# Softmax with a relative position bias, streamed through SBUF: chunks of 7 rows in three buffers and a 3-row spare instead of chunks of 6 rows in four

## The chip, the cores and the metric

The kernel runs on one core of a Trainium2 chip. The metric is the device time of one execution in microseconds, given as the median of several runs. The profile is a record of one execution, taken by the hardware profiler.

## What is computed

```python
B, H, S, max_rel = 2, 8, 2112, 16
rel = clip(pos[:, None] - pos[None, :], -max_rel, max_rel) + max_rel
logits = logits + rel_bias[:, rel][None]          # (B, H, S, S) float32
exp = np.exp(logits - logits.max(axis=-1, keepdims=True))
return exp / exp.sum(axis=-1, keepdims=True)      # (B, H, S, S) float32
```

To every row of a 2112 x 2112 matrix of logits a bias is added that depends only on the distance between row and column, and each row then goes through a softmax. There are 16 such matrices, 285 MB of input and as much of output.

## The kernel before

**Layout.** The 2 x 8 x 2112 rows are shared out over 128 partitions: `ROWS = 264` consecutive rows to each. A row has `S = 2112` float32 numbers, 8,448 bytes. A chunk is `R = 6` rows of every partition (6,336 KB in all, 50,688 contiguous bytes per partition), held in one of `NBUF = 4` buffers `X0` to `X3`. There are 44 chunks; chunk n lives in buffer n mod 4, and it is computed in place and stored from the same buffer.

**The bias.** ACT's DMA queue loads the table `rel_bias`, broadcast to all partitions (L97, 132 KB, into F). VectorE selects each partition's head and builds from it the long strip `M` in PSUM (L118 to L155). The bias of one row is a window of `M` that slides by one element from row to row. Once per round of four chunks VectorE copies the part of `M` that the round needs into the tile `F` in SBUF (`strip`, L160), and the adds read shifted windows of `F`.

**VectorE.** For each chunk it waits for the load's semaphore and then runs for each row one custom operation (L166): it adds the bias and leaves the negative maximum of the row. Then it waits for the exponentials of half a chunk, takes the reciprocals of their sums (L183) and scales the rows (L187), half a chunk at a time. It does not begin the next chunk's adds before that.

**ScalarE** computes the exponential of each row with the sum of the row beside it (L175), as soon as the row is added.

**SP** issues all large transfers, on one DMA queue, in a fixed order: at the start the first chunk as six transfers of one row (L88; five of them count on the semaphore `pre`, for which VectorE waits before the first `strip`, L190), and three whole chunks; then store 0; then in a loop for each chunk

```python
store(j + (b + 1) * R, (b + 1) % NBUF)   # waits until the rows of that chunk are scaled
take(nc.sync, st[b], 16)                 # waits until the store before it has landed
load(j + (b + NBUF) * R, b)              # into the buffer that came free
```

so the load of chunk c+4 goes out once store c has landed and store c+1 has been issued. At the end three stores, the last chunk's in two halves of 3 rows, and a wait for all of them. Line L74 is the helper `take`, through which all engines wait, L78 the helper `load`, L82 the helper `store`.

Of the kernel before, what the change touches and what calls it, by code (L numbers as in the profile page):

```python
# [7 lines left out]
FP32 = mybir.dt.float32  # L8
I32 = mybir.dt.int32
EXP = mybir.ActivationFunctionType.Exp  # L10
ALU = mybir.AluOpType
ENG = mybir.EngineType
# [3 lines left out]
def kernel(  # L16
# [6 lines left out]
    nc = tc.nc  # L23
    P = 128
    B, H, S, S2 = logits.shape
# [3 lines left out]
    ROWS = B * H * S // P  # L29
    PB = S // ROWS  # L30
    assert ROWS * P == B * H * S and PB * ROWS == S and PB == H == 8
    R = 6
    NBUF = 4
    STEP = R * NBUF
    N = ROWS // R
    HALF = R // 2
    assert ROWS % STEP == 0
    MW = S + ROWS - 1
    FW = S + STEP - 1
    BIG = 3.0e38  # L40

    io = ctx.enter_context(tc.tile_pool(name="io", bufs=1))
    X = [io.tile([P, R * S], FP32, tag=f"X{b}", name=f"X{b}") for b in range(NBUF)]
    F = io.tile([P, FW], FP32, tag="F", name="F")
    rbS = io.tile([P, W], FP32, tag="rbS", name="rbS")
    nmax = io.tile([P, STEP], FP32, tag="nmax", name="nmax")
    tot = io.tile([P, STEP], FP32, tag="tot", name="tot")
    rec = io.tile([P, STEP], FP32, tag="rec", name="rec")
    ip = io.tile([P, 3, PB], I32, tag="ip", name="ip")
    ps = ctx.enter_context(tc.tile_pool(name="ps", bufs=1, space=bass.MemoryType.PSUM))  # L50
    M = ps.tile([P, 4096], FP32, tag="M", name="M")

    def view(t, offset, dims):

        return bass.AP(tensor=t.tensor, offset=t.offset + offset, ap=[[list(t.ap[0])[0], P]] + dims)

    def rows(t, j, n):

        return bass.AP(tensor=t.tensor, offset=t.offset + j * S, ap=[[ROWS * S, P], [1, n * S]])

    with tc.tile_critical(no_gpsimd_drain=True):
        ld = [nc.alloc_semaphore(f"ld{b}") for b in range(NBUF)]
        st = [nc.alloc_semaphore(f"st{b}") for b in range(NBUF)]
        added = nc.alloc_semaphore("added")
        expd = nc.alloc_semaphore("expd")
        scaled = nc.alloc_semaphore("scaled")
        inv = nc.alloc_semaphore("inv")
        rb = nc.alloc_semaphore("rb")
        pre = nc.alloc_semaphore("pre")
        idx = nc.alloc_semaphore("idx")  # L70
        dve = nc.alloc_semaphore("dve")

        def take(eng, sem, n):
            eng.wait_ge(sem, n).then_inc(sem, -n)  # L74


        def load(j, b):
            nc.sync.dma_start(out=X[b][:, :], in_=rows(logits, j, R)).then_inc(ld[b], 16)  # L78

        def store(j, b, s0=0, n=R):  # L80
            take(nc.sync, scaled, n)
            nc.sync.dma_start(  # L82
                out=rows(out, j + s0, n), in_=X[b][:, s0 * S : (s0 + n) * S]
            ).then_inc(st[b], 16)


        for r in range(R):
            nc.sync.dma_start(  # L88
                out=X[0][:, r * S : (r + 1) * S], in_=rows(logits, r, 1)
            ).then_inc(ld[0] if r == R - 1 else pre, 16)  # L90
        for n in range(1, NBUF):
            load(n * R, n)

        rbB = view(F, 0, [[1, H * W]])
        nc.scalar.dma_start(  # L97
            out=rbB,
            in_=bass.AP(tensor=rel_bias.tensor, offset=rel_bias.offset, ap=[[0, P], [1, H * W]]),
# [4 lines left out]
        v = nc.vector  # L104
        done = [0]

        def then(ins):
            done[0] += 1
            ins.then_inc(dve, 1)

        def settle():
            v.wait_ge(dve, done[0])

        SC = H * W
        mask = [F[:, SC + i * PB : SC + (i + 1) * PB] for i in range(9)]
        dp, dh, eq, hm, gt, le, lt, ra, rz = mask
        v.wait_ge(idx, 2)
        then(v.tensor_scalar(out=ip[:, 1], in0=ip[:, 0], scalar1=3, scalar2=7,  # L118
                             op0=ALU.logical_shift_right, op1=ALU.bitwise_and))
# [7 lines left out]
        for m, op in ((eq, ALU.is_equal), (gt, ALU.is_gt), (le, ALU.is_le), (lt, ALU.is_lt)):  # L127
# [3 lines left out]
        then(v.tensor_tensor(  # L131
            out=view(F, 0, [[W, H], [1, W]]), in0=view(F, 0, [[W, H], [1, W]]),
            in1=view(F, SC + 3 * PB, [[1, H], [0, W]]), op=ALU.mult))
        settle()
        then(v.tensor_reduce(out=rbS[:, :], in_=view(F, 0, [[1, W], [W, H]]),  # L135
                             axis=mybir.AxisListType.X, op=ALU.add))
        settle()
# [3 lines left out]
        then(v.tensor_tensor(  # L141
            out=view(F, 0, [[W, PB], [1, W]]), in0=view(F, SC + 2 * PB, [[1, PB], [0, W]]),
            in1=view(rbS, W - 1, [[0, PB], [-1, W]]), op=ALU.mult))
# [6 lines left out]
            out=view(M, U, [[ROWS, PB], [1, W]]), in0=view(F, 0, [[W, PB], [1, W]]),  # L150
            in1=view(F, SC + 8 * PB, [[1, PB], [0, W]]), op=ALU.add))
        then(v.tensor_copy(out=view(M, U + W, [[ROWS, PB], [1, ROWS - W]]),  # L152
                           in_=view(F, SC + 7 * PB, [[1, PB], [0, ROWS - W]])))
# [1 line left out]
        then(v.tensor_copy(out=M[:, U + PB * ROWS : MW], in_=high.to_broadcast([P, MW - U - PB * ROWS])))  # L155
        settle()

        def strip(j):

            v.tensor_copy(out=F[:, :], in_=M[:, bass.ds(ROWS - STEP - j, FW)]).then_inc(dve, 1)  # L160

        def add(b):
            take(v, ld[b], 16)
            for r in range(b * R, (b + 1) * R):
                x = X[b][:, (r - b * R) * S : (r - b * R + 1) * S]
                v.tensor_tensor_reduce(  # L166
                    out=x, in0=x, in1=F[:, STEP - 1 - r : STEP - 1 - r + S], scale=-1.0, scalar=BIG,
                    op0=ALU.add, op1=ALU.min, accum_out=nmax[:, r : r + 1],
                ).then_inc(added, 1)

        def exps(b):
            for r in range(b * R, (b + 1) * R):
                x = X[b][:, (r - b * R) * S : (r - b * R + 1) * S]
                take(nc.scalar, added, 1)
                nc.scalar.activation(  # L175
                    out=x, in_=x, func=EXP, scale=-1.0, bias=nmax[:, r : r + 1],
                    accum_out=tot[:, r : r + 1],
                ).then_inc(expd, 1)

        def scale(b):  # L180
            for r0 in range(b * R, (b + 1) * R, HALF):
                take(v, expd, HALF)
                v.reciprocal(out=rec[:, r0 : r0 + HALF], in_=tot[:, r0 : r0 + HALF]).then_inc(inv, 1)  # L183
                take(v, inv, 1)
                for r in range(r0, r0 + HALF):
                    x = X[b][:, (r - b * R) * S : (r - b * R + 1) * S]
                    v.tensor_scalar_mul(out=x, in0=x, scalar1=rec[:, r : r + 1]).then_inc(scaled, 1)  # L187

        v.sem_inc(dve, -done[0])
        take(v, pre, 16 * (R - 1))  # L190
        with nc.Fori(0, ROWS - STEP + 1, STEP, engines=[ENG.DVE]) as j:  # L191
            strip(j)
            take(v, dve, 1)
            for b in range(NBUF):
                add(b)
                scale(b)
        with nc.Fori(0, ROWS // STEP, 1, engines=[ENG.Activation]):
            for b in range(NBUF):
                exps(b)

        store(0, 0)
        with nc.Fori(0, ROWS - 2 * STEP + 1, STEP, engines=[ENG.SP]) as j:
            for b in range(NBUF):
                store(j + (b + 1) * R, (b + 1) % NBUF)
                take(nc.sync, st[b], 16)
                load(j + (b + NBUF) * R, b)
        for n in range(N - NBUF + 1, N - 1):
            store(n * R, n % NBUF)  # L210
        store((N - 1) * R, (N - 1) % NBUF, 0, HALF)
        store((N - 1) * R, (N - 1) % NBUF, HALF, R - HALF)
        for b in range(NBUF):
            take(nc.sync, st[b], 32 if b == (N - 1) % NBUF else 16)


# [28 lines left out]
```

## Time and profile before

| | |
|---|---|
| median of 3 runs | 1330.84 us (1330.0 to 1331.05) |
| span of the profiled execution | 1327.7 us |
| median less this span | 3.1 us |
| VectorE busy | 976.6 us (74%) |
| ScalarE busy | 575.2 us (43%) |
| read and written in HBM | 285.61 and 285.47 MB, 430 GB/s over the span |
| packets on all DMA queues | 13,683 |

The profile's times are microseconds from the start of the span. DVE is VectorE, ACT ScalarE, SPq and ACTq are the sequencers that issue transfers. A line of the timeline gives start, duration, engine, line of code, operation, output and input, and in brackets how long the engine was idle before it and what ended that. A line on a DMA queue gives its packets, its megabytes and the time its packets took as a share of 16 engines' time. A line of a window gives the window, its length, busy time of VectorE, ScalarE and GpSimd, the TensorE clock, the share of busy DMA engines and GB/s. TensorE is not used.

### The profile page before, as it was taken

Reading aid. Unit: us, or ns where it says so; the run is one execution under the profiler, and the core shown is the slowest. Engines: PE = TensorE matmul, PEld = TensorE weight load, DVE = VectorE, ACT = ScalarE, POOL = GpSimd, SP = SyncE. Lnnn points to the kernel's source line nnn. Section 1 sums busy time; section 2 is a strip of 40 time slices with the busy share of each in tenths; the row PEclk is TensorE's granted clock in tenths of the full one; section 3 lists DMA queues with packets and bytes.
Section 4 is the critical chain, followed back from the end, with each engine's and each line's share of the span. In section 5 each row is a group of like instructions: output and inputs, shape, how many; then the busy total and the mean of one; then the engine's idle time right before and its main releaser. Section 6 shows DMA issues by size and latency. Waiting matters only on the chain. (4 is left out here: it accounts for less than half of the span.)

```text
span 1327.7 us, 2454 instructions
## 1 busy us (share of the span) xinstructions
DVE 976.6 (74%) x911; ACT 575.2 (43%) x539; POOL 0.4 (0%) x6
## 2 busy tenths in 40 slices
DVE  6999667777777776687778777677877776687772
ACT  2564333444444343345444333444444343335440
POOL 0000000000000000000000000000000000000000
DMA  9999999999999999999999999999999999999998
GB/s 392 431 428 437 435 420 437 435 434 425 435 437 434 428 435 434 435 429 429 438 438 432 426 438 437 437 425 437 437 437 425 435 440 437 428 432 438 437 426 359
DMA packets 13683, 571.11 MB, mean 430 GB/s; under 512 B 1521, under 2 KB 1649, under 8 KB 1649
## 3 DMA queue, kind: packets, MB, share of 16 engines
q1 hardware_dynamic: 13536, 570.96, 99.6%
q10 hardware_dynamic: 144, 0.14, 0.1%
q14 instruction: 3, 0.02, 0.0%
HBM read 285.61 MB, written 285.47 MB: 430 GB/s over the span
## 5 line engine op out<-in xcount | busy, mean ns | idle before, releaser
L166 DVE CUSTOM_DVE_ANT_0 X<-X,F 128x2112 f32<-128x2112 f32 x264 | 605.2, 2354 | 301.3 <-DVEq L74 301.3
L175 ACT ACTIVATE X<-X,nmax 128x2112 f32<-128x2112 f32 x264 | 541.7, 2052 | 539.3 <-ACTq L74 517.6
L187 DVE TENSOR_SCALAR X<-X,rec 128x2112 f32<-128x2112 f32 x264 | 332.4, 1315 | 13.2
L175 ACT ACT_TABLE_LOAD x11 | 14.1, 1283 | 183.3 <-ACTq L74 183.3
L175 ACT ACTIVATION_READ_ACCUMULATOR X<-X,nmax 128x1 f32 x264 | 49.2, 186 | 0.0
L160 DVE COPY F<-M 128x2135 f32 x11 | 26.1, 2374 | 6.3 <-DVEq L74 6.3
L166 DVE DVE_READ_ACCUMULATOR2_ANT nmax<- 128x1 f32 x264 | 21.7, 82 | 0.0
L183 DVE RECIPROCAL rec<-tot 128x3 f32<-128x3 f32 x88 | 14.9, 170 | 0.0
L131 DVE TENSOR_TENSOR F<-F 128x264 f32<-128x264 f32 x1 | 0.4, 434 | 4.7 <-DMA F<-in_rel_bias_dram 4.7
L152 DVE COPY M<-F 128x1848 f32<-128x1848 f32 x1 | 2.1, 2077 | 0.0
L118 DVE TENSOR_SCALAR ip<-ip 128x8 int32<-128x8 int32 x1 | 0.2, 173 | 1.3 <-POOL ip L102 1.3
L135 DVE TENSOR_REDUCE rbS<-F 128x33 f32<-128x264 f32 x1 | 0.6, 610 | 0.0
L149 DVE TENSOR_TENSOR M<-F 128x264 f32<-128x264 f32 x1 | 0.4, 441 | 0.0
L141 DVE TENSOR_TENSOR F<-F,rbS 128x264 f32<-128x264 f32 x1 | 0.4, 425 | 0.0
L128 DVE TENSOR_SCALAR F<-F 128x8 f32<-128x8 f32 x4 | 0.4, 166 | 0.0
L154 DVE COPY M<-rbS 128x247 f32<-128x247 f32 x1 | 0.4, 408 | 0.0
L139 DVE TENSOR_SCALAR F<-F,rbS 128x8 f32<-128x8 f32 x1 | 0.2, 231 | 0.0
L145 DVE SCALAR_TENSOR_TENSOR F<-F,rbS 128x8 f32<-128x8 f32 x1 | 0.2, 225 | 0.0
L140 DVE TENSOR_SCALAR F<-F,rbS 128x8 f32<-128x8 f32 x1 | 0.2, 222 | 0.0
L146 DVE SCALAR_TENSOR_TENSOR F<-F,rbS 128x8 f32<-128x8 f32 x1 | 0.2, 219 | 0.0
L124 DVE TENSOR_TENSOR F<-ip 128x8 f32<-128x8 int32 x1 | 0.2, 167 | 0.0
L121 DVE TENSOR_TENSOR F<-ip 128x8 f32<-128x8 int32 x1 | 0.2, 166 | 0.0
(9 smaller groups left out, 1.2 us busy)
## 6 DMA issues: line engine op xcount, KB each, us to landing
X<-in_logits_dram SPq DMA_DIRECT2D x43, 6336.0 KB, 44.6
out_dram<-X SPq DMA_DIRECT2D x43, 6336.0 KB, 52.6
X<-in_logits_dram SPq DMA_DIRECT2D x6, 1056.0 KB, 12.1
out_dram<-X SPq DMA_DIRECT2D x2, 3168.0 KB, 21.1
F<-in_rel_bias_dram ACTq DMA_DIRECT2D x1, 132.0 KB, 6.2
```

Of the source, the lines that this page charges most:

```text
L128: then(v.tensor_scalar(out=m, in0=dp, scalar1=0.0, scalar2=None, op0=op))
L131: then(v.tensor_tensor(out=view(F, 0, [[W, H], [1, W]]), in0=view(F, 0, [[W, H], [1, W]]), in1=view(F, SC + 3 * PB, [[1, H], [0, W]]), op= ...
L135: then(v.tensor_reduce(out=rbS[:, :], in_=view(F, 0, [[1, W], [W, H]]), axis=mybir.AxisListType.X, op=ALU.add))
L141: then(v.tensor_tensor(out=view(F, 0, [[W, PB], [1, W]]), in0=view(F, SC + 2 * PB, [[1, PB], [0, W]]), in1=view(rbS, W - 1, [[0, PB], [-1, ...
L149: then(v.tensor_tensor(out=view(M, U, [[ROWS, PB], [1, W]]), in0=view(F, 0, [[W, PB], [1, W]]), in1=view(F, SC + 8 * PB, [[1, PB], [0, W]] ...
L152: then(v.tensor_copy(out=view(M, U + W, [[ROWS, PB], [1, ROWS - W]]), in_=view(F, SC + 7 * PB, [[1, PB], [0, ROWS - W]])))
L154: then(v.tensor_copy(out=M[:, 0:U], in_=low.to_broadcast([P, U])))
L160: v.tensor_copy(out=F[:, :], in_=M[:, bass.ds(ROWS - STEP - j, FW)]).then_inc(dve, 1)
L166: v.tensor_tensor_reduce(out=x, in0=x, in1=F[:, STEP - 1 - r : STEP - 1 - r + S], scale=-1.0, scalar=BIG, op0=ALU.add, op1=ALU.min, accum_ ...
L175: nc.scalar.activation(out=x, in_=x, func=EXP, scale=-1.0, bias=nmax[:, r : r + 1], accum_out=tot[:, r : r + 1],).then_inc(expd, 1)
L183: v.reciprocal(out=rec[:, r0 : r0 + HALF], in_=tot[:, r0 : r0 + HALF]).then_inc(inv, 1)
L187: v.tensor_scalar_mul(out=x, in0=x, scalar1=rec[:, r : r + 1]).then_inc(scaled, 1)
```

## The change

A chunk is 7 rows (7,392 KB, 59,136 bytes per partition), and there are three buffers for it, plus a spare `XS` of 3 rows; the four tiles together take as much of SBUF as before. 36 chunks of 7 rows cover 252 rows; the last 12 rows are chunks of 6 (buffer 0), 3 (the spare) and 3 (buffer 1). The first chunk is loaded in one transfer, and the semaphore `pre` with VectorE's wait on it is gone. `strip` runs once per round of three chunks, and once more before the last 12 rows. A chunk of 7 is scaled in parts of 4 and 3 rows. SP's loop keeps its order, so the load of chunk c+3 goes out once store c has landed and store c+1 has been issued.

```diff
-    R = 6
-    NBUF = 4
+    R = 7
+    NBUF = 3
     STEP = R * NBUF
-    N = ROWS // R
-    HALF = R // 2
+    N = ROWS // STEP * NBUF
+    SPARE = 3
+    LAST = [(N * R, 6, 0, 0), (N * R + 6, 3, NBUF, 6), (N * R + 9, 3, 1, 9)]
+    PARTS = [(0, 4), (4, 3)]
...
+    X.append(io.tile([P, SPARE * S], FP32, tag="XS", name="XS"))
...
-        for r in range(R):
-            nc.sync.dma_start(
-                out=X[0][:, r * S : (r + 1) * S], in_=rows(logits, r, 1)
-            ).then_inc(ld[0] if r == R - 1 else pre, 16)
-        for n in range(1, NBUF):
+        for n in range(NBUF):
             load(n * R, n)
...
         v.sem_inc(dve, -done[0])
-        take(v, pre, 16 * (R - 1))
-        with nc.Fori(0, ROWS - STEP + 1, STEP, engines=[ENG.DVE]) as j:
-            strip(j)
-            take(v, dve, 1)
+        with nc.Fori(0, N * R - STEP + 1, STEP, engines=[ENG.DVE]) as j:
+            strip(bass.ds(ROWS - STEP - j, FW))
             for b in range(NBUF):
-                add(b)
-                scale(b)
+                add(b, R, b * R, STEP - 1)
+                scale(b, PARTS, b * R)
+        strip(slice(0, FW))
+        for j, n, b, r0 in LAST:
+            add(b, n, r0, ROWS - 1 - N * R)
+            scale(b, [(i, 3) for i in range(0, n, 3)], r0)
...
         store(0, 0)
-        with nc.Fori(0, ROWS - 2 * STEP + 1, STEP, engines=[ENG.SP]) as j:
+        with nc.Fori(0, N * R - 2 * STEP + 1, STEP, engines=[ENG.SP]) as j:
             for b in range(NBUF):
                 store(j + (b + 1) * R, (b + 1) % NBUF)
                 take(nc.sync, st[b], 16)
                 load(j + (b + NBUF) * R, b)
-        for n in range(N - NBUF + 1, N - 1):
-            store(n * R, n % NBUF)
-        store((N - 1) * R, (N - 1) % NBUF, 0, HALF)
-        store((N - 1) * R, (N - 1) % NBUF, HALF, R - HALF)
-        for b in range(NBUF):
-            take(nc.sync, st[b], 32 if b == (N - 1) % NBUF else 16)
+        store((N - 2) * R, (N - 2) % NBUF)
+        for j, n, b, r0 in LAST:
+            if b < NBUF:
+                take(nc.sync, st[b], 16)
+            load(j, b, n)
+        store((N - 1) * R, (N - 1) % NBUF)
+        for j, n, b, r0 in LAST:
+            store(j, b, n)
+        for b in range(NBUF + 1):
+            take(nc.sync, st[b], 16)
```

More of the change, by code (lines that the diff above doesn't have):

```diff
@@ L31 @@
     assert ROWS * P == B * H * S and PB * ROWS == S and PB == H == 8
-    R = 6
-    NBUF = 4
+    R = 7
+    NBUF = 3
     STEP = R * NBUF
-    N = ROWS // R
-    HALF = R // 2
-    assert ROWS % STEP == 0
+    N = ROWS // STEP * NBUF
+    SPARE = 3
+    LAST = [(N * R, 6, 0, 0), (N * R + 6, 3, NBUF, 6), (N * R + 9, 3, 1, 9)]
+    assert N * R + 12 == ROWS
+    PARTS = [(0, 4), (4, 3)]
     MW = S + ROWS - 1
@@ L61 @@
     with tc.tile_critical(no_gpsimd_drain=True):
-        ld = [nc.alloc_semaphore(f"ld{b}") for b in range(NBUF)]
-        st = [nc.alloc_semaphore(f"st{b}") for b in range(NBUF)]
+        ld = [nc.alloc_semaphore(f"ld{b}") for b in range(NBUF + 1)]
+        st = [nc.alloc_semaphore(f"st{b}") for b in range(NBUF + 1)]
         added = nc.alloc_semaphore("added")
@@ L68 @@
         rb = nc.alloc_semaphore("rb")
-        pre = nc.alloc_semaphore("pre")
         idx = nc.alloc_semaphore("idx")
@@ L74, in take, with load, store @@
             eng.wait_ge(sem, n).then_inc(sem, -n)
-        def load(j, b):
-            nc.sync.dma_start(out=X[b][:, :], in_=rows(logits, j, R)).then_inc(ld[b], 16)
-        def store(j, b, s0=0, n=R):
+        def load(j, b, n=R):
+            nc.sync.dma_start(out=X[b][:, 0 : n * S], in_=rows(logits, j, n)).then_inc(ld[b], 16)
+        def store(j, b, n=R):
             take(nc.sync, scaled, n)
-            nc.sync.dma_start(
-                out=rows(out, j + s0, n), in_=X[b][:, s0 * S : (s0 + n) * S]
-            ).then_inc(st[b], 16)
-        for r in range(R):
-            nc.sync.dma_start(
-                out=X[0][:, r * S : (r + 1) * S], in_=rows(logits, r, 1)
-            ).then_inc(ld[0] if r == R - 1 else pre, 16)
-        for n in range(1, NBUF):
+            nc.sync.dma_start(out=rows(out, j, n), in_=X[b][:, 0 : n * S]).then_inc(st[b], 16)
+        for n in range(NBUF):
             load(n * R, n)
@@ L156, with strip, add @@
         settle()
-        def strip(j):
-            v.tensor_copy(out=F[:, :], in_=M[:, bass.ds(ROWS - STEP - j, FW)]).then_inc(dve, 1)
-        def add(b):
+        def strip(start):
+            v.tensor_copy(out=F[:, :], in_=M[:, start]).then_inc(dve, 1)
+            take(v, dve, 1)
+        def add(b, n, r0, top):
             take(v, ld[b], 16)
-            for r in range(b * R, (b + 1) * R):
-                x = X[b][:, (r - b * R) * S : (r - b * R + 1) * S]
+            for i in range(n):
+                x = X[b][:, i * S : (i + 1) * S]
@@ L166, in add, with exps @@
                 v.tensor_tensor_reduce(
-                    out=x, in0=x, in1=F[:, STEP - 1 - r : STEP - 1 - r + S], scale=-1.0, scalar=BIG,
-                    op0=ALU.add, op1=ALU.min, accum_out=nmax[:, r : r + 1],
+                    out=x, in0=x, in1=F[:, top - r0 - i : top - r0 - i + S], scale=-1.0, scalar=BIG,
+                    op0=ALU.add, op1=ALU.min, accum_out=nmax[:, r0 + i : r0 + i + 1],
                 ).then_inc(added, 1)
-        def exps(b):
-            for r in range(b * R, (b + 1) * R):
-                x = X[b][:, (r - b * R) * S : (r - b * R + 1) * S]
+        def exps(b, n, r0):
+            for i in range(n):
+                x = X[b][:, i * S : (i + 1) * S]
@@ L174, in exps, with scale @@
                 take(nc.scalar, added, 1)
                 nc.scalar.activation(
-                    out=x, in_=x, func=EXP, scale=-1.0, bias=nmax[:, r : r + 1],
-                    accum_out=tot[:, r : r + 1],
+                    out=x, in_=x, func=EXP, scale=-1.0, bias=nmax[:, r0 + i : r0 + i + 1],
+                    accum_out=tot[:, r0 + i : r0 + i + 1],
                 ).then_inc(expd, 1)
[L180 to L183, printed above, removed]
-                take(v, inv, 1)
-                for r in range(r0, r0 + HALF):
-                    x = X[b][:, (r - b * R) * S : (r - b * R + 1) * S]
-                    v.tensor_scalar_mul(out=x, in0=x, scalar1=rec[:, r : r + 1]).then_inc(scaled, 1)
+        def scale(b, parts, r0):
+            for i0, n in parts:
+                take(v, expd, n)
+                c = slice(r0 + i0, r0 + i0 + n)
+                v.reciprocal(out=rec[:, c], in_=tot[:, c]).then_inc(inv, 1)
+                take(v, inv, 1)
+                for i in range(i0, i0 + n):
+                    x = X[b][:, i * S : (i + 1) * S]
+                    v.tensor_scalar_mul(
+                        out=x, in0=x, scalar1=rec[:, r0 + i : r0 + i + 1]
+                    ).then_inc(scaled, 1)
@@ L189 @@
         v.sem_inc(dve, -done[0])
-        take(v, pre, 16 * (R - 1))
-        with nc.Fori(0, ROWS - STEP + 1, STEP, engines=[ENG.DVE]) as j:
-            strip(j)
-            take(v, dve, 1)
+        with nc.Fori(0, N * R - STEP + 1, STEP, engines=[ENG.DVE]) as j:
+            strip(bass.ds(ROWS - STEP - j, FW))
             for b in range(NBUF):
-                add(b)
-                scale(b)
-        with nc.Fori(0, ROWS // STEP, 1, engines=[ENG.Activation]):
+                add(b, R, b * R, STEP - 1)
+                scale(b, PARTS, b * R)
@@ L198 @@
+        strip(slice(0, FW))
+        for j, n, b, r0 in LAST:
+            add(b, n, r0, ROWS - 1 - N * R)
+            scale(b, [(i, 3) for i in range(0, n, 3)], r0)
+        with nc.Fori(0, N // NBUF, 1, engines=[ENG.Activation]):
             for b in range(NBUF):
-                exps(b)
+                exps(b, R, b * R)
+        for j, n, b, r0 in LAST:
+            exps(b, n, r0)
         store(0, 0)
-        with nc.Fori(0, ROWS - 2 * STEP + 1, STEP, engines=[ENG.SP]) as j:
+        with nc.Fori(0, N * R - 2 * STEP + 1, STEP, engines=[ENG.SP]) as j:
@@ L208 @@
                 load(j + (b + NBUF) * R, b)
-        for n in range(N - NBUF + 1, N - 1):
-            store(n * R, n % NBUF)
-        store((N - 1) * R, (N - 1) % NBUF, 0, HALF)
-        store((N - 1) * R, (N - 1) % NBUF, HALF, R - HALF)
-        for b in range(NBUF):
-            take(nc.sync, st[b], 32 if b == (N - 1) % NBUF else 16)
+        store((N - 2) * R, (N - 2) % NBUF)
[4 more added lines that the diff above has]
+        store((N - 1) * R, (N - 1) % NBUF)
+        for j, n, b, r0 in LAST:
+            store(j, b, n)
+        for b in range(NBUF + 1):
+            take(nc.sync, st[b], 16)
 _INS = ['logits', 'rel_bias']
```

## The prediction

> **What bounds the kernel now.** I read the page's span and DMA parts first, then the timeline in the middle of the run, the transfers by line, the timeline of the first 100 us, and the DMA queues asked for two short windows near the start.
>
> ```profile
> span 1327.7 us, 2454 instructions
> ...
> DMA  9999999999999999999999999999999999999998
> ...
> q1 hardware_dynamic: 13536, 570.96, 99.6%
> ```
>
> The 16 DMA engines carry 571 MB on SP's queue (q1) and their packets fill 99.6% of the span. All the traffic is the input read once and the output written once, so neither VectorE nor ScalarE sets the time. An edit can matter here only where it leaves the DMA queue empty, or where it changes what a packet costs. The span is 1327.7 us, the median of the runs 1330.84 us, so 3.1 us lie outside the span; I add what changes inside the span to the median.
>
> The timeline in the middle, and the transfers by line (the last column is the median time from issue to landing):
>
> ```profile
> 908.12 0.35 SPq L78 DMA_DIRECT2D X<-in_logits_dram  x1
> ...
> 922.97 2.36 DVE L166 CUSTOM_DVE_ANT_0 X<-X,F 128x2112 f32<-128x2112 f32 x1 [8.09 <-DVEq L74]
> ...
> 945.00 0.34 SPq L82 DMA_DIRECT2D out_dram<-X  x1
> ...
> 952.93 2.36 DVE L166 CUSTOM_DVE_ANT_0 X<-X,F 128x2112 f32<-128x2112 f32 x1 [5.87 <-DVEq L74]
> ```
>
> ```profile
> X<-in_logits_dram SPq DMA_DIRECT2D x43, 6336.0 KB, 44.6
> out_dram<-X SPq DMA_DIRECT2D x43, 6336.0 KB, 52.6
> ```
>
> A load issued at 908.12 lands 44.6 us later, at 952.7, and VectorE starts on it at 952.93 after idling 5.87 us. One transfer of 6 rows occupies the engines for 14.94 us (below), so a load stands behind two earlier transfers and a store behind two and a half: with four buffers the queue is always deep.
>
> **The head.** The timeline of the first 100 us, then the six single-row loads and the bias load, line by line:
>
> ```profile
> 0.92 0.41 ACTq L97 DMA_DIRECT2D F<-in_rel_bias_dram  x1
> 0.97 3.34 SPq L88 DMA_DIRECT2D X<-in_logits_dram  x6
> ...
> 7.16 0.43 DVE L131 TENSOR_TENSOR F<-F 128x264 f32<-128x264 f32 x1 [4.69 <-DMA F<-in_rel_bias_dram]
> ...
> 18.48 2.38 DVE L160 COPY F<-M 128x2135 f32 x1 [6.26 <-DVEq L74]
> 21.17 2.36 DVE L166 CUSTOM_DVE_ANT_0 X<-X,F 128x2112 f32<-128x2112 f32 x1 [0.31 <-DVEq L74]
> ...
> 35.17 3.78 DVE L187 TENSOR_SCALAR X<-X,rec 128x2112 f32<-128x2112 f32 x3
> ...
> 42.88 2.35 DVE L166 CUSTOM_DVE_ANT_0 X<-X,F 128x2112 f32<-128x2112 f32 x1
> 43.07 22.23 SPq L82 DMA_DIRECT2D out_dram<-X  x2
> ...
> 45.16 2.35 DVE L166 CUSTOM_DVE_ANT_0 X<-X,F 128x2112 f32<-128x2112 f32 x1
> ...
> 64.58 2.35 DVE L166 CUSTOM_DVE_ANT_0 X<-X,F 128x2112 f32<-128x2112 f32 x1
> ...
> 81.12 0.36 SPq L78 DMA_DIRECT2D X<-in_logits_dram  x1
> ...
> 96.06 0.35 SPq L78 DMA_DIRECT2D X<-in_logits_dram  x1
> ```
>
> ```profile
> L88 SPq DMA_DIRECT2D X<-in_logits_dram x6: 388/488/707, 1.0 to 3.7; - x6
> ...
> DMA to landing us min/median/max: 6.8/12.1/16.9
> ```
>
> The load at 81.12 is released by the landing of store 0, the one at 96.06 by store 1: 14.94 us per transfer of 6 rows, 2.49 us a row, 17.43 us for 7 rows. The last single row lands at 3.7 + 16.9 = 20.6. A chunk of 6 costs VectorE 64.58 - 42.88 = 21.70 us; a further row adds one add (45.16 - 42.88 = 2.28) and one scale (3.78 / 3 = 1.26), so 25.2 us for 7 rows. SP issues a store some 0.4 us after the chunk ends (the second of the two stores from 43.07 ends at 65.30 and takes 0.34).
>
> **Part 1, the steady state: nothing.** With three buffers the queue's order is store c, load c+2, store c+1, load c+3, 17.43 us each. After load c+1 has landed, store c and load c+2 keep the engines busy for 34.9 us. Store c+1 is issued 25.2 + 0.4 us after that landing and starts a few us later, so it is queued 6 to 8 us before the engines would run dry; SP then finds store c landed and issues load c+3 at once. Behind SP's wait for the scaling stands only that load. VectorE's refill of F once per round falls into its idle 9.7 us per chunk (34.9 - 25.2). If that cover went, each missing us would cost 33 us (33 store-and-load pairs in SP's loop); that is a rival.
>
> **Part 2, the first round: a gap of about 1 us.** SP issues store 1 before it waits for store 0 and loads chunk 3. Before, the queue held 24 rows ahead of store 0; now 21. Count from the first add, close behind the landing of chunk 0. The two other loads and store 0 take 3 x 17.43 = 52.3 us; store 1 is issued after 2 x 25.2 + 0.4 = 50.8 us. So it comes 1.5 us before the queue is empty, and a transfer issued into an empty queue needs a start of its own. Before has such a start only at the program's beginning: the first row lands 6.8 us after its issue, 2.5 of them its transfer, so 4.3 is the upper end. From below:
>
> ```profile
> 0.00:2.00 2.00, 0.63 (x5) 0.00 (x0) 0.42 (x6) 1.00 0.00 2
> ```
>
> With the issue at 0.97 nothing of weight moves before 2.00 (2 GB/s in this window), so at least 1.0. I take 2.5, since the upper end is a read that shares its start with the bias. The gap is 2.5 - 1.5 = 1.0 us, 0 to 2.8. [...]
>
> **Part 3, the first load as one transfer: the bias comes late.** The bias row (132 KB, ACT's queue q10) is issued beside the first load, and VectorE's preparation of the mask waits for it. The packets of the two queues in 0 to 3 us, then in 3 to 6 us:
>
> ```profile
> q1 hardware_dynamic: 15, 0.13, 28.4%
> q10 hardware_dynamic: 50, 0.05, 8.6%
> ```
>
> ```profile
> q1 hardware_dynamic: 76, 0.64, 65.0%
> q10 hardware_dynamic: 74, 0.08, 14.3%
> ```
>
> After a few bias packets that go ahead, the engines take one packet of each queue in turn, 76 against 74. The bias has 144 packets, nine per engine (eight of data, one semaphore); 50 are gone by 3 us, the other 94 are six per engine. So each engine moves about six packets of logits before the bias is through. Those packets hold one row of one partition now, 2.49 / 8 = 0.31 us each; after the change 7 rows, 2.18 us each. The bias then lands 6 x 1.87 = 11.2 us later, at 7.1 + 11.2 = 18.3 instead of 7.16. What hung on it was hidden behind the load until now (VectorE waits 6.26 us for rows at 18.48). Mask preparation and F take 7.9 us more (7.16 to the wait at 12.2, some 0.1 to begin, then 18.48 to 21.17), so the first add starts at 26.2. The load itself, 20.6 + 2.49 less some 0.2 of Part 4, lands at 22.9 and no longer ends last. Everything VectorE does in the first round is 3.3 us later, store 1 with it: issued at 26.2 + 50.8 = 77.0, while store 0 lands at 22.9 + 52.3 = 75.2. The gap in the queue grows to 77.0 + 2.5 - 75.2 = 4.3 us. Store 0 itself (26.2 + 25.6 = 51.8 plus a start of 2.5) is still in time for the end of the loads near 57.8. From then on Part 1 holds: the queue never makes up lost time. Bounds: nothing of the bias is late (gap 1.0), or all nine packets alternate (another 5.6, gap 9.9).
>
> **Part 4, fewer packets: -0.3 us.** 94 transfers become 78, at 144 packets each 13,536 become 11,232. No row prices a packet alone; the single rows at 0.31 us each show that seven times the size is nothing like seven times cheaper. I take -0.3, from -1 to 0.
>
> **Part 5, the end: nothing.** Of the last loads (6, 3 into the spare, 3) two go out once store 33 has landed, the third once store 34 has. From load 35's landing: store 34 and the three loads last 17.4 + 29.9 = 47.3 us; store 35 is ready at 25.6. The chunk of 6 is computed from 32.4 to 54.1, needed at 64.8; the two of 3 (13.3 us each: three adds, the last exp, three scales) at 67.4 and 80.7, needed at 79.7 and 87.2. Both kernels end with a store of 3 rows.
>
> **Sum:** +4.3 - 0.3 = +4.0 us: 1330.84 + 4.0 = 1334.8 us.
>
> **Rivals.** *A, the bias still comes early (not slower).* If a queue's turn is a whole group of packets and not one, the bias leaves in its first turn, lands near 7, and the gap is Part 2's alone: 1.0 - 0.3 = +0.7, 1331.5 us. It decides below a bias landing of 22.9 - 7.9 = 15.0; above, every us costs a us. Against it stand 76 and 74. [...] Chance 0.2.
>
> *B, the queue runs dry in every round.* It would need a chunk to take over 32 us from landing to queued store where I count 28. Each us short costs 33 us, so 1 us gives 1368 us. For it: the margin is a fifth of a round, where it was two transfers; against it: 25.2 is from steady rows. Chance 0.04.
>
> *C, the engines no longer drift apart.* The loads issued first, 17 intervals later and 20 after that:
>
> ```profile
> 126.28 0.35 SPq L78 DMA_DIRECT2D X<-in_logits_dram  x1
> ...
> 638.99 0.35 SPq L78 DMA_DIRECT2D X<-in_logits_dram  x1
> ...
> 1237.05 0.35 SPq L78 DMA_DIRECT2D X<-in_logits_dram  x1
> ```
>
> Early, a round took 512.71 / 17 = 30.16 us, late 598.06 / 20 = 29.90: 17 x 0.26 = 4.4 us lost in the first half, of unknown cause. If new sizes and a common restart at 77 us avoid it, the result is 4.0 - 4.4 = -0.4, 1330.4 us, and with A 1327.1; it may as well grow. Chance 0.1.
>
> **Numbers.** 0.2% (2.7 us) is about what a measurement of this kernel can tell from no change. My forecast has 0.66; with its bounds (start 1.0 to 4.3, bias from five to nine packets, the drift some 2 us either way) it lies over +2.7 in about six of seven cases, 0.56. B adds 0.04, A's upper end 0.03: slower 0.63. Same takes most of A, the lower end of the forecast and part of C: 0.29. Faster is left 0.08. The range, 1330.5 to 1339.5, reaches to A below and nearly to the nine packets above; B and C with A lie outside.
>
> **What would show it.** Right: the line of the bias load takes 15 to 20 us to land; F's refill follows the mask preparation without a wait for rows; the first add starts at 25 to 28; DMA share dips between 75 and 81 us and nowhere else; later rounds take 34.9 us. Wrong: a bias landing near 7 (A), idle DMA in every round (B), early rounds as short as late ones (C).

## The result and the profile after

| | before | after |
|---|---|---|
| median of 4 runs | 1330.42 us (1329.31 to 1331.05) | 1344.40 us (1342.80 to 1344.92) |
| span of the profiled execution | 1327.7 us | 1342.5 us |

The change makes the kernel slower: the ratio is 1.0104 (95% interval 1.0091 to 1.0116), 14.0 us. The forecast was 1334.8, in a range that ended at 1339.5.

The page of after, with the same lines as before:

```profile
span 1342.5 us, 2371 instructions
...
DMA  9999999999999999999999999999999999999997
...
q1 hardware_dynamic: 11232, 570.95, 99.2%
```

The DMA engines are still shown busy nearly everywhere. Whatever costs 14 us, the page's shares hide most of it. Its list of transfers shows how short the queue has become: a store lands 27.0 us after its issue, where before took 52.6.

```profile
out_dram<-X SPq DMA_DIRECT2D x36, 7392.0 KB, 27.0
```

**The head.** The timeline's first 101 us, then the bias in the list of transfers (last column: issue to landing):

```profile
16.61 0.43 DVE L124 TENSOR_TENSOR F<-F 128x264 f32<-128x264 f32 x1 [14.15 <-DMA F<-in_rel_bias_dram]
...
24.84 2.36 DVE L160 CUSTOM_DVE_ANT_0 X<-X,F 128x2112 f32<-128x2112 f32 x1 [0.32 <-DVEq L76]
...
50.25 25.72 SPq L84 DMA_DIRECT2D out_dram<-X  x2
...
76.23 0.35 SPq L80 DMA_DIRECT2D X<-in_logits_dram  x1
```

```profile
F<-in_rel_bias_dram ACTq DMA_DIRECT2D x1, 132.0 KB, 15.7
```

The bias lands at 16.61 instead of 7.16, and VectorE waits 14.15 us for it. Mask and strip follow without a wait for rows, and the first add starts at 24.84. Times to landing of the transfers of these lines: of the three first loads, of stores 0 and 1, and of the load issued at 76.23:

```profile
DMA to landing us min/median/max: 22.2/39.2/56.2
```

```profile
DMA to landing us min/median/max: 19.9/22.6/25.3
```

```profile
DMA to landing us min/median/max: 38.0/38.0/38.0
```

The first load lands at 0.96 + 22.2 = 23.2. Store 0 is issued at 50.25 and lands 25.3 us later, at 75.6, just as store 1 goes out (50.25 + 25.72 - 0.36 = 75.6). The queue is empty then. Store 1 needs 19.9 us where a transfer in a full queue takes 17.44: a gap of 2.5 us. The next load lands at 76.23 + 38.0 = 114.2, 18.7 us after store 1, another 1.3 us late. Head: 3.8 us. Only the 2.5 us are a gap, though: in experiment 4, which has none, the same load (issued at 75.82) also comes late, 18.4 us after the store before it.

**The rounds.** Three loads of after, 12 and 17 rounds apart, and the same window of both kernels (the last column is GB/s), before first:

```profile
175.63 0.35 SPq L80 DMA_DIRECT2D X<-in_logits_dram  x1
...
600.37 0.35 SPq L80 DMA_DIRECT2D X<-in_logits_dram  x1
...
1200.71 0.35 SPq L80 DMA_DIRECT2D X<-in_logits_dram  x1
```

```profile
700.00:1000.00 300.00, 222.75 (x205) 131.10 (x123) 0.00 (x0) 1.00 1.00 435
```

```profile
700.00:1000.00 300.00, 212.92 (x193) 122.50 (x115) 0.00 (x0) 1.00 1.00 428
```

The kernel before settled at 29.90 us a round in its second half, which is 34.89 for 7 rows. After takes 424.74 / 12 = 35.40 early and 600.34 / 17 = 35.31 late: the loss never stops. Over these 29 rounds it is 1025.08 - 29 x 34.89 = 13.3 us, against 4.4 us in before's first half and nothing later. That is 8.9 us more; with the head's 3.8 it makes 12.7 of the 14.8 us between the spans, and the rest falls after 1200 us, most of it one more late load. In the slow window the engines count as busy (1.00) and move less (428 against 435 GB/s): single packets take longer. In the packet records 394 of 9,216 packets of 59,136 bytes lie more than 0.06 us above their usual 2.18 us, some 200 of them after 700 us; before, 100 of 11,008 lay as much above 1.87, and 3 of them after 700 us. The slow packets belong to loads: from 100 us on a store of after lands 17.4 to 17.5 us behind the transfer ahead of it, a load 17.4 to 19.0 us.

**A theory.** The 16 engines finish their parts of one transfer at different times. In the single engines' landing events (16 per transfer in the trace, printed by no view) the first and the last engine are 1 us apart early, and in before the spread grows to 5.6 us by 550 us and stays; there the slow packets stop. In after it grows to 7 to 8.7 us and then falls back again and again. One such place: the first engine finishes a load at 1024.3, the last at 1033.0, and the store that follows goes out only here:

```profile
1023.86 0.34 SPq L84 DMA_DIRECT2D out_dram<-X  x1
```

That is 9.1 us before the last engine is through and 0.5 us before the first one is. The first engine finishes its part of the store at 1043.3, 19.0 us after the load instead of 17.4, which fits a stop of 1.5 us. About every second round is like this. Of the 15 stores issued between 700 and 1201 us, 7 went out 0.5 to 1.8 us before the first engine was through: that engine took 17.8 to 19.0 us to the end of its part, and the load behind each of the 7 was slow as well (17.8 to 19.0 us from the last engine's landing of the store to its landing of the load). The other 8 went out 2.0 to 2.3 us before, and they and the loads behind them took 17.4 to 17.6 us. The two kinds take turns because a slow load leaves the next store more time (9.6 to 10.8 us before the last engine is through, instead of 9.1 to 9.3). Theory D (depth): the short queue holds the leaders (the engines that are ahead), lines the engines up again, and the slow packets go on. Theory S (size): larger packets meet slow packets whatever the queue holds.

### The profile page after: what moved, and what is told of

Read it like the earlier page. It is cut to its first block, busy times and chain, and to the rows that moved or that the text cites. A ratio compares the mean times of both kernels' runs of the same rounds, so it can differ in the third digit from the quotient of the medians.

```text
span 1342.5 us, 2371 instructions
## 1 busy us (share of the span) xinstructions
DVE 978.7 (73%) x901; ACT 575.9 (43%) x540; POOL 0.4 (0%) x6
## 5 line engine op out<-in xcount | busy, mean ns | idle before, releaser
L160 DVE CUSTOM_DVE_ANT_0 X<-X,F 128x2112 f32<-128x2112 f32 x261 | 597.8, 2354 | 315.6 <-DVEq L76 315.6
L169 ACT ACTIVATE X<-X,nmax 128x2112 f32<-128x2112 f32 x261 | 535.4, 2052 | 492.4 <-ACTq L76 471.8
L182 DVE TENSOR_SCALAR X<-X,rec 128x2112 f32<-128x2112 f32 x261 | 327.6, 1315 | 11.2
L153 DVE COPY F<-M 128x2132 f32 (+1 forms) x13 | 30.8, 2369 | 0.5 <-DVEq L186 0.5
L178 DVE RECIPROCAL rec<-tot 128x4 f32<-128x4 f32 (+1 forms) x76 | 13.0, 171 | 4.8 <-DVEq L76 4.8
L169 ACT ACTIVATE XS<-XS,nmax 128x2112 f32<-128x2112 f32 x3 | 6.2, 2055 | 8.4 <-ACTq L76 8.2
L160 DVE CUSTOM_DVE_ANT_0 XS<-XS,F 128x2112 f32<-128x2112 f32 x3 | 6.9, 2352 | 0.0
L182 DVE TENSOR_SCALAR XS<-XS,rec 128x2112 f32<-128x2112 f32 x3 | 3.8, 1316 | 0.1
```

The lines of the kernel that those rows point to most:

```text
L153: v.tensor_copy(out=F[:, :], in_=M[:, start]).then_inc(dve, 1)
L160: v.tensor_tensor_reduce(out=x, in0=x, in1=F[:, top - r0 - i : top - r0 - i + S], scale=-1.0, scalar=BIG, op0=ALU.add, op1=ALU.min, accum_ ...
L169: nc.scalar.activation(out=x, in_=x, func=EXP, scale=-1.0, bias=nmax[:, r0 + i : r0 + i + 1], accum_out=tot[:, r0 + i : r0 + i + 1],).then ...
L178: v.reciprocal(out=rec[:, c], in_=tot[:, c]).then_inc(inv, 1)
L182: v.tensor_scalar_mul(out=x, in0=x, scalar1=rec[:, r0 + i : r0 + i + 1]).then_inc(scaled, 1)
```

## The experiments

All were compared with the kernel before on the same chip; the ratios are to it.

**1. Bias ahead of the loads (in the changed kernel).**

```diff
+        nc.sync.dma_start(out=rbB, in_=...rel_bias...).then_inc(rb, 16)
         for n in range(NBUF):
             load(n * R, n)
-        nc.scalar.dma_start(out=rbB, in_=...rel_bias...).then_inc(rb, 16)
```

> The changed kernel with one edit: the bias load goes out on SP's queue ahead of the first chunk instead of on ACT's queue beside it. Both theories of the rest agree here: the bias lands near 3 to 5 us instead of 16.6, the first add starts when the load has landed (23.2 instead of 24.84), and the gap in the queue near 75 us shrinks by that 1.7 us, from 3.8 to about 2. Expected 1342.5 us (1341.5 to 1343.5). If the late bias had cost all of the forecast's 3.3 us, 1341; if none, 1344.4.

Measured: 1341.06 us (1331.11 to 1343.19), ratio 1.0062 (1.0038 to 1.0086). Its timeline, and the landing of store 1:

```profile
5.46 0.43 DVE L124 TENSOR_TENSOR F<-F 128x264 f32<-128x264 f32 x1 [3.00 <-DMA F<-in_rel_bias_dram]
...
23.61 2.36 DVE L160 CUSTOM_DVE_ANT_0 X<-X,F 128x2112 f32<-128x2112 f32 x1 [10.24 <-DVEq L76]
...
49.03 25.73 SPq L84 DMA_DIRECT2D out_dram<-X  x2
```

```profile
DMA to landing us min/median/max: 20.4/20.4/20.4
```

The bias no longer delays anything: VectorE waits 10.24 us for rows, and store 1 goes out 1.2 us earlier, at 74.4, to land at 94.8 instead of 95.5. The load behind it lands at 114.4, no earlier than in after (114.2), so by this trace the late bias costs next to nothing in the end; the expected gain of 1.7 us is not there. The median is 3.3 us lower and just below the expected range, but of the nine runs two took 1331 to 1332 us, one 1337, the others 1340.75 to 1343.19. Why some runs escape the loss is not shown. Neither theory had foreseen that.

**2. Stores in two parts, queued earlier (in the changed kernel).**

```diff
-            take(nc.sync, scaled, n)
-            nc.sync.dma_start(out=rows(out, j, n), in_=X[b][:, 0 : n * S]).then_inc(st[b], 16)
+            for s0, m in PARTS if n == R else [(0, n)]:
+                take(nc.sync, scaled, m)
+                nc.sync.dma_start(out=rows(out, j + s0, m), in_=X[b][:, s0 * S : (s0 + m) * S]).then_inc(st[b], 16)
```

> The changed kernel with one edit: each store of 7 rows goes out as two transfers, of 4 and 3 rows, each as soon as its rows are scaled, so that the queue is fed some 4 us earlier in every round. Theory D (depth: the leading DMA engines run the short queue empty, are held and lined up again, and the slow packets of the first half never stop): the leaders are no longer held, slow packets stop after the first 500 us, 1344.4 - 8 = 1336 us (1334 to 1339). Theory S (size: packets of 59,136 bytes meet slow packets whatever the queue): 1344 us or a little more for the added transfers.

Measured: 1335.51 us (1333.93 to 1338.11), ratio 1.0042 (1.0026 to 1.0059). Two loads of it, 17 rounds apart (the second is that of the last 6 rows):

```profile
632.95 0.35 SPq L80 DMA_DIRECT2D X<-in_logits_dram  x1
...
1226.55 0.37 SPq L80 DMA_DIRECT2D X<-in_logits_dram  x1
```

593.60 / 17 = 34.92 us a round: the late loss is gone, with packets of 59,136 bytes in every load and all of VectorE's work in place. This speaks for D.

**3. Six rows in three buffers (the changed kernel with R = 6).**

```diff
-    R = 7
+    R = 6
...
-    PARTS = [(0, 4), (4, 3)]
+    PARTS = [(0, 3), (3, 3)]
```

> The changed kernel with chunks of 6 rows in its three buffers (14 rounds of three, then 6, 3 and 3 rows): packets as large as before the change, the queue as short as after it. The first round has its gap as well (some 3.5 us). Theory D (depth): the leaders are held in every round and the slow packets go on, 1330.4 + 3.5 + 6 or more: 1340 us or above. Theory S (size): the drift stops as before the change, 1334 us (1332 to 1336).

Measured: 1347.54 us (1346.71 to 1349.68), ratio 1.0130 (1.0113 to 1.0147). Two loads, 20 rounds apart:

```profile
607.86 0.35 SPq L80 DMA_DIRECT2D X<-in_logits_dram  x1
...
1215.88 0.35 SPq L80 DMA_DIRECT2D X<-in_logits_dram  x1
```

30.40 us a round where the same packets in four buffers take 29.90. The size of before with the depth of after is the slowest of all; S falls. Seven rows are better than six in three buffers, which fits that they leave VectorE more time per round: from 600 us on the stores go out 9.1 to 10.8 us before the last engine is through, here 7.7 to 9.1.

**4. Scaling cut to 64 of 2112 elements (in the changed kernel).**

```diff
-                    x = X[b][:, i * S : (i + 1) * S]
+                    x = X[b][:, i * S : i * S + 64]
                     v.tensor_scalar_mul(
```

> The changed kernel with the scaling cut to the first 64 of a row's 2112 elements (the rest of the row is stored unscaled): all transfers, sizes and buffers stay, only VectorE is some 7 us faster per chunk, so stores are queued 7 us earlier. The gap near 75 us goes away (3.8 us). Theory D (depth): the slow packets also stop after the first half, 1344.4 - 3.8 - 8 = 1332 us (1330 to 1335). Theory S (size): 1344.4 - 3.8 = 1340.5 us.

Measured: 1329.16 us (1328.24 to 1331.09), ratio 0.9992 (0.9982 to 1.0001). Its first stores and loads of the rounds, and two loads 17 rounds apart (the second is that of the last 6 rows):

```profile
63.78 0.36 SPq L84 DMA_DIRECT2D out_dram<-X  x1
75.82 0.35 SPq L80 DMA_DIRECT2D X<-in_logits_dram  x1
...
623.78 0.35 SPq L80 DMA_DIRECT2D X<-in_logits_dram  x1
...
1216.47 0.37 SPq L80 DMA_DIRECT2D X<-in_logits_dram  x1
```

Store 1 is in the queue at 63.78, 12 us ahead of store 0's landing, so there is no gap, and the rounds take 592.69 / 17 = 34.86 us. Same buffers, same transfers, same sizes: VectorE, about a quarter idle in both kernels, is what made the changed one slow, through the moment at which its stores enter the queue. A rival would be that VectorE's own traffic in SBUF slows the packets; it falls by experiment 2, where the late loss goes while VectorE does all its work, and by experiment 5, where it comes while VectorE does what it did before. The measured time lies below the range that D gave; its middle, 1332, was 3 us too high.

**5. The kernel before with a shorter queue.**

```diff
         store(0, 0)
+        store(R, 1)
...
-                store(j + (b + 1) * R, (b + 1) % NBUF)
+                store(j + (b + 2) * R, (b + 2) % NBUF)
                 take(nc.sync, st[b], 16)
                 load(j + (b + NBUF) * R, b)
```

> The kernel before with one edit in SP's order: the load of chunk c+4 goes out after store c+2 instead of after store c+1. Chunks, buffers, tiles and packets stay as they were; only the queue is one transfer shorter, and the first round has no gap (store 2 is issued at 87 us, the queue lasts to 90). Theory D (depth): the leading DMA engines run dry in every round as in the three-buffer kernel with 6 rows, 1347.5 less its gap of some 3.7: 1344 us (1340 to 1346). Rival: what slows the changed kernel is something else of its layout (three buffers, rounds of 21 or 18 rows, the remainder of 12 rows); then 1330.4 us as before.

Measured: 1344.58 us (1341.40 to 1346.21), ratio 1.0114 (1.0097 to 1.0131). Two loads, 20 rounds apart:

```profile
602.60 0.35 SPq L78 DMA_DIRECT2D X<-in_logits_dram  x1
...
1205.95 0.35 SPq L78 DMA_DIRECT2D X<-in_logits_dram  x1
```

30.17 us a round, against 29.90, in the fastest of its four runs. The rounds are slow again by SP's order alone, with nothing else of the change, and the rival falls. Not all of the 14.7 us between the medians is this loss, though. At the end of the same execution:

```profile
1295.21 30.90 SPq L82 DMA_DIRECT2D out_dram<-X  x3
```

```profile
1318.00:1322.00 4.00, 3.85 (x5) 1.93 (x2) 0.00 (x0) 1.00 0.00 0
```

After its last load only one store was left in the queue. It lands at 1318.7, while VectorE still works on the last chunk, and the DMA engines stand still until the next store at 1321.76. The last stores land 4.5 us later for it, a loss that after does not have. It was not foreseen, and that the median met the expected 1344 is in part luck.

**6. Scaling cut to half (in the changed kernel):** as in 4, with 1056 instead of 64.

> The changed kernel with the scaling cut to the first 1056 of a row's 2112 elements (the rest is stored unscaled): stores are queued some 4 us earlier per chunk, half of what the cut to 64 elements gave, with the same transfers. Theory D with a threshold: the leading engines get 4 us more, some 11 us ahead of the last, which the drift of 6 to 7 us does not reach, so they are never held: as with 64 elements, 1329 to 1331 us. Rival D2: the loss falls in step with the time at which the store is queued: half way between 1344.4 and 1329.2, 1336 to 1338 us.

Measured: 1331.39 us (1330.05 to 1335.85) beside 1331.66 for the kernel before on that chip, ratio 1.0000 (0.9990 to 1.0010). Three loads, 8 and 8 rounds apart:

```profile
626.46 0.35 SPq L80 DMA_DIRECT2D X<-in_logits_dram  x1
...
907.25 0.35 SPq L80 DMA_DIRECT2D X<-in_logits_dram  x1
...
1186.17 0.35 SPq L80 DMA_DIRECT2D X<-in_logits_dram  x1
```

280.79 / 8 = 35.10 us a round, then 278.92 / 8 = 34.87. D2, with its 1336 to 1338, falls: half of experiment 4's cut already brings the time back to that of the kernel before. In the landing events the stores from 600 us on go out 13.0 us or more before the last engine is through (9.1 or more in after, 15.0 in experiment 4) and at least 4.4 us before the first one. The spread grows to 8.6 us, as in after, but here it stays, and no load is slow after 900 us.

**7. The kernel before, first chunk in one transfer.**

```diff
-        for r in range(R):
-            nc.sync.dma_start(out=X[0][:, r * S : (r + 1) * S], ...)
-        for n in range(1, NBUF):
+        for n in range(NBUF):
             load(n * R, n)
...
-        take(v, pre, 16 * (R - 1))
```

> The kernel before with its first chunk loaded in one transfer (and the wait on the single rows gone). The bias is expected to land near 14 to 15 us instead of 7.16 and the first add at 22 to 23 instead of 21.17. With four buffers the queue holds 24 rows and store 1 is issued at 67 us against store 0's landing at 81, so nothing of it reaches the end: 1330.4 us (1329.5 to 1331). If the late bias costs by itself, 1332 us.

Measured: 1330.85 us (1329.12 to 1332.40), ratio 1.0002 (0.9992 to 1.0011).

```profile
16.23 0.43 DVE L127 TENSOR_TENSOR F<-F 128x264 f32<-128x264 f32 x1 [13.78 <-DMA F<-in_rel_bias_dram]
...
24.47 2.36 DVE L162 CUSTOM_DVE_ANT_0 X<-X,F 128x2112 f32<-128x2112 f32 x1 [0.32 <-DVEq L74]
```

The bias is as late as in after, and it costs nothing: with four buffers the queue covers it.

**8. Both repairs: bias first and stores in parts (in the changed kernel),** the edits of 1 and 2.

> The changed kernel with both edits: bias ahead of the loads on SP's queue, and stores of 7 rows as 4 and 3. Theory D: the leaders are not held, and the first round has no gap with either edit alone, so bias first adds nothing to the split stores: 1335 us (1332 to 1336). If the edits add up (1.7 and 9), 1333.8.

Measured: 1334.11 us (1332.08 to 1341.60), ratio 1.0044 (1.0024 to 1.0063). The interval holds both expectations, 1335 and 1333.8; it doesn't tell them apart. Two of the seven runs took 1338.71 and 1341.60 us; why is not shown.

**9. Four buffers of 6 rows, with bias first, one first transfer, and stores in halves.** The edits of 7 and 1, and the store split at 3 rows.

> A version that takes what helped and leaves what hurt: four buffers of 6 rows, first chunk in one transfer, bias ahead of it on SP's queue, every store in two halves of 3 rows as soon as they are scaled. The queue is even deeper than before, but before has no idle engine to win back beyond its drift of the first half: 1330 us (1328 to 1331.5).

Measured: 1333.55 us (1332.44 to 1336.33), ratio 1.0031 (1.0019 to 1.0044): slower than before, a miss. No version here with the whole computation beats the kernel before.

**10. The kernel before with stores in halves alone.**

> The kernel before with every store in two halves of 3 rows, each as soon as it is scaled, and nothing else. It asks what a split store costs where the queue is deep anyway. If the 1333.6 of the four-buffer version with split stores comes from the split: 1333 us (1332 to 1334.5). If it comes from the bias on SP's queue or the first transfer: 1330.4.

Measured: 1336.14 us (1334.84 to 1337.64) beside 1331.66, ratio 1.0034 (1.0023 to 1.0046). Three loads, 17 and 20 rounds apart:

```profile
126.67 0.35 SPq L78 DMA_DIRECT2D X<-in_logits_dram  x1
...
642.95 0.35 SPq L78 DMA_DIRECT2D X<-in_logits_dram  x1
...
1243.58 0.35 SPq L78 DMA_DIRECT2D X<-in_logits_dram  x1
```

30.37 us a round early and 30.03 late, against 30.16 and 29.90: split stores alone cost some 4.5 us for 43 more transfers (0.1 us each on average), more than expected. Whether that is a price of each transfer is open: the spread of the engines also grew, to 10 us, and 157 of 5,504 load packets were slow, where before had 100 among 11,008 of loads and stores. Of the 11,264 store packets only 2 were slow. The cost fits the miss of 9, and that 2 and 8 stop near 1335 while 4 and 6 get back to the kernel before.

## Why the prediction was right or wrong

- **The direction and the head were right, for the smaller part of the loss.** The forecast had the bias at 18.3, the first add at 26.2, store 1 at 77.0 and a gap of 4.3 us; the trace has 16.6, 24.84, 75.6 and 2.5 us. The start of a transfer into an empty queue, taken as 2.5 between 1.0 and 4.3, measured 2.5. That the head's 3.8 us come close to 4.3 is luck: 1.3 of them are a late load, which was not foreseen. Of the 14 us the forecast had the cause of 2.5.
- **Rival A fell.** The bias landed at 16.6, not near 7. Neither after nor experiment 7 shows it leaving in one turn, and the chance of 0.2 for that was the author's estimate; the trace has 87 bias packets beside 102 of logits between 3 and 18 us. But the landing did not grow in step with the packets either: 16.2 with 6-row packets (experiment 7), 16.6 with 7. In after 64 bias packets, four per engine, went ahead, and the other five took turns with logits; in experiment 7 it was 48, three and six. The forecast had counted six turns.
- **Part 1 was the step that failed.** "The steady state: nothing" measured 8.9 us. Its sign, later rounds of 34.9 us, came out as 35.3 to 35.4. It counted a lead of 6 to 8 us for a single queue and took any lead above zero as enough. The stores of the rounds do go out 9 to 11 us before the last engine is through, and for it that is enough. The first engine is up to 8.7 us ahead of the last, so from 700 us on it has the store only 0.5 to 2.3 us before it runs dry, too little for the start of a transfer in 7 of 15 rounds. The prediction's own rival C had the engines drifting apart, and rival B had the lead, but the two were never set against each other: B was priced for all engines running dry (33 us per us short) and given 0.04, C for a drift that may vanish, with "some 2 us either way" as the size of its growth.
- **The idle-cover argument was read from the wrong side.** VectorE's idle 9.7 us per chunk stood as the cover; experiments 4 and 6 show that shortening VectorE's work removes the whole loss. An engine at 73% busy, waiting for loads in nearly every round, set the time at which the stores went out, and with it the loss.
- **Part 4, fewer packets,** cannot be seen: merging six transfers into one is worth nothing measurable (experiment 7); by experiment 10's average of 0.1 us a transfer, 16 fewer would be worth 1.6 us, an estimate that no run tests. **Part 5** was right to within a microsecond: the last 38 rows, from the landing of the last load of 7 rows at 1245.7 us on, land in 95.6 us, where 38 rows at the pace of before's second half take 94.7.
- **What stays open.** Experiments 2, 4, 5 and 6 show that the lead at which stores enter the queue decides, and experiments 2 and 3 that size does not. That the leaders' stop is what lets the slow packets go on is read from landing events, where each stop is followed by a slow load, and from experiment 6, which has neither; no run sets the stop alone. Why a load's packets are slow behind such a stop and in the first 500 us of before and after, and why some runs of experiment 1 escaped, is not known.

## What to carry to other kernels

The saturated DMA queue of this kernel was 16 engines that drifted apart. Before shortening such a queue, set the time by which the next transfer is queued against the spread of the engines (here 6 to 9 us) and the start of a transfer (here 2.5 us at store 1, and some 2 us for the first engine in the rounds), not against zero. The 99% busy of a page tells nothing of it. The page's time from issue to landing does (27.0 us less the transfer's own 17.4 is a lead of 9.6), and so does the period between a loop's own issues. When a kernel bound by transfers slows down, try first to make the compute between load and store shorter, even by leaving some of it out: here that told a late store from a slower transfer in one run.

## What the runs showed of the hardware

- The engines' spread grew to 5.6 us in the kernel before and to 7 to 8.7 us after. Where the leaders were not held, slow packets all but ended once the spread stood still: 5.6 us in before (434 to 435 GB/s from 700 us on), 6.1 in experiment 4, 8.6 in experiment 6.
- Slow packets were nearly all in loads: 157 of the load's packets and 2 of the stores' in experiment 10.
- A small transfer on a second queue waited for the large packets beside it: 132 KB took 6.2 us beside packets of 8,448 bytes, 15.7 us beside packets of 59,136, and 4.5 us ahead of them on their own queue (experiment 1).
- Two transfers in place of one cost some 0.1 us more on average, with the queue never empty (experiment 10).
